# Softmax-gradient kernel on one core: a longer y buffer with the two groups of a pair shifted by 3840 columns, and ScalarE's row sum in one in-place instruction

## The chip, the cores and the metric

The kernel runs on one core of one Trainium2 chip. The metric is the device time of one execution in microseconds (us); smaller is better. Before the change the median was 1867.82 us in three runs (1866.99 to 1868.07).

Some words first. A *DMA* moves data between HBM (the main memory) and SBUF (on-chip memory); 16 DMA engines carry it in *packets* of 32 or 64 KB. A DMA *lands* when its completion reaches those who wait for it. VectorE and ScalarE do the arithmetic; SyncE only issues the DMAs. PSUM is a second on-chip memory, to which the old sum writes.

## The reference

```python
# y, dy: float32 [8, 1024, 8192]
softmax_x = np.exp(y)
sum_dy = np.sum(dy, axis=-1, keepdims=True)
return dy - softmax_x * sum_dy
```

There are 8192 rows of 8192 numbers. Each output element needs one exp, one multiply and one add; each row of dy must be summed first. y and dy are each read once (268.4 MB each), the output is written once (268.4 MB).

## The kernel before

A *group* is 128 partitions with two rows (R = 2) of 8192 columns each: 8 MB of dy in a tile `x`, 8 MB of y in `y_t`. The loop takes a *pair* of groups: two `x` tiles and a single `y_t`, which the first group fills with one load and the second with two loads, one a row, as the first group's arithmetic releases the columns. There are 16 pairs. Every DMA is issued by SyncE on one queue, in program order, and each waits on SyncE for what it depends on.

```python
    PIECES = [(0, 2048), (2048, 5120), (5120, D)]          # D = 8192
    x_ts = [pool.tile([P, W], fp32, name=f"x{j}") for j in range(2)]   # W = 2 * D
    y_t = pool.tile([P, W], fp32, name="y_t")
    copied = psum.tile([P, H], fp32, name="copied")         # H = D // 2, in PSUM

    def sums(x):                  # row 0 on VectorE, row 1 on ScalarE, in two halves
        ...
        nc.vector.tensor_reduce(out=s_t[:, 0:1], in_=x[:, :D], ..., negate=True)
        for h in range(2):
            nc.scalar.activation(
                copied[:], x[:, D + h * H : D + (h + 1) * H], COPY, accum_out=half_t[:, h : h + 1]
            )
        nc.vector.tensor_scalar(...)          # -(half 0 + half 1)
        return s_t

    def compute(x, s_t, r):       # one row, in three pieces
        for b, e in PIECES:
            cs = slice(r * D + b, r * D + e)
            nc.scalar.activation(y_t[:, cs], y_t[:, cs], EXP)
            nc.vector.scalar_tensor_tensor(out=x[:, cs], in0=y_t[:, cs],
                scalar=s_t[:, r : r + 1], in1=x[:, cs], op0=ALU.mult, op1=ALU.add)

    for g in range(0, G, 2):
        load_dy(g, x_ts[0])
        load_y(g, 0, W)
        s_t = sums(x_ts[0])
        for r in range(R):
            compute(x_ts[0], s_t, r)
        load_dy(g + 1, x_ts[1])
        s_t = sums(x_ts[1])
        for r in range(R):
            load_y(g + 1, r * D, (r + 1) * D)
            compute(x_ts[1], s_t, r)
        for j in range(2):
            nc.sync.dma_start(out=out_v[g + j], in_=x_ts[j][:])
```

Of the kernel before, what the change touches and what calls it, by code (L numbers as in the profile page):

```python
# [1 line left out]

# [5 lines left out]


EXP = mybir.ActivationFunctionType.Exp  # L10
COPY = mybir.ActivationFunctionType.Copy
ALU = mybir.AluOpType


@with_exitstack
def kernel(
    ctx: ExitStack,
    tc: tile.TileContext,
    y: bass.AP,
    dy: bass.AP,  # L20
    out: bass.AP,
):




    nc = tc.nc
    P = nc.NUM_PARTITIONS
    fp32 = mybir.dt.float32

    N, D = y.flatten_outer_dims().shape
    R = 2
    W = R * D
    G = N // (P * R)
    assert N == G * P * R and D == 8192 and G % 2 == 0
    H = D // 2

    PIECES = [(0, 2048), (2048, 5120), (5120, D)]

    y_v = y.flatten_outer_dims().rearrange("(g p r) d -> g p (r d)", p=P, r=R)  # L40
    dy_v = dy.flatten_outer_dims().rearrange("(g p r) d -> g p (r d)", p=P, r=R)
    out_v = out.flatten_outer_dims().rearrange("(g p r) d -> g p (r d)", p=P, r=R)

    pool = ctx.enter_context(tc.tile_pool(name="pool", bufs=1))
    stats = ctx.enter_context(tc.tile_pool(name="stats", bufs=3))
    psum = ctx.enter_context(tc.tile_pool(name="psum", bufs=1, space=bass.MemoryType.PSUM))
    x_ts = [pool.tile([P, W], fp32, name=f"x{j}") for j in range(2)]
    y_t = pool.tile([P, W], fp32, name="y_t")
    copied = psum.tile([P, H], fp32, name="copied")

    def load_dy(g, x):
        nc.sync.dma_start(out=x[:], in_=dy_v[g])  # L52

    def sums(x):
        s_t = stats.tile([P, R], fp32, name="s_t")
        half_t = stats.tile([P, 2], fp32, name="half_t")
        nc.vector.tensor_reduce(  # L57
            out=s_t[:, 0:1], in_=x[:, :D], axis=mybir.AxisListType.X, op=ALU.add, negate=True
        )
        for h in range(2):  # L60
            nc.scalar.activation(  # L61
                copied[:], x[:, D + h * H : D + (h + 1) * H], COPY, accum_out=half_t[:, h : h + 1]
            )
        nc.vector.tensor_scalar(  # L64
            out=s_t[:, 1:2],
            in0=half_t[:, 0:1],
            scalar1=half_t[:, 1:2],
            scalar2=-1.0,
            op0=ALU.add,
            op1=ALU.mult,  # L70
        )
        return s_t

    def load_y(g, lo, hi):
        nc.sync.dma_start(out=y_t[:, lo:hi], in_=y_v[g][:, lo:hi])  # L75

    def compute(x, s_t, r):
        for b, e in PIECES:
            cs = slice(r * D + b, r * D + e)
            nc.scalar.activation(y_t[:, cs], y_t[:, cs], EXP)  # L80
            nc.vector.scalar_tensor_tensor(  # L81
                out=x[:, cs],
                in0=y_t[:, cs],
                scalar=s_t[:, r : r + 1],
                in1=x[:, cs],
                op0=ALU.mult,
                op1=ALU.add,
            )

    for g in range(0, G, 2):  # L90
        load_dy(g, x_ts[0])
        load_y(g, 0, W)
        s_t = sums(x_ts[0])
        for r in range(R):
            compute(x_ts[0], s_t, r)
        load_dy(g + 1, x_ts[1])
        s_t = sums(x_ts[1])
        for r in range(R):
            load_y(g + 1, r * D, (r + 1) * D)
            compute(x_ts[1], s_t, r)  # L100
        for j in range(2):
            nc.sync.dma_start(out=out_v[g + j], in_=x_ts[j][:])


# [1 line left out]
_INS = ['y', 'dy']  # L106
_OUTS = [((8, 1024, 8192), 'float32')]


# [23 lines left out]
```

## Time and profile before

| what | before |
|---|---|
| median time | 1867.8 us |
| bytes moved | 805.37 MB, mean 432 GB/s |
| DMA queue busy, of 16 engines' span | 99.9% |
| VectorE (DVE), ScalarE (ACT) busy | 46%, 37% |
| period of one pair (from one load of the first x to the next) | 116.2 us |

These are lines of the page of the kernel before: the span, the busy engines, the rate in 40 equal slices of the span, the DMA queue with packets, MB and the share of 16 engines' time that its packets took, then the two lines of the chain that ended last (by engine, by tile), and last the DMA issues with their median us from issue to landing.

```profile
span 1865.9 us, 923 instructions
DVE 859.8 (46%) x256; ACT 698.7 (37%) x321; POOL 0.2 (0%) x4
...
GB/s 427 424 430 427 430 447 427 427 431 445 427 427 441 426 437 434 438 431 427 437 438 429 433 428 440 434 431 437 425 438 436 433 436 425 439 433 436 434 428 391
...
q1 hardware_dynamic: 16128, 805.31, 99.9%
...
DMA 64%; DVE 13%; ACT 10%; another core or an unknown queue 9%; issue 1%; SPq 0%; DVEq 0%; ACTq 0%
...
y_t<-in_y_dram SPq DMA_DIRECT2D x32, 4096.0 KB, 18.1
```

Two lines compete for the reader's belief. The queue line says that the DMA engines were busy for all but 0.1% of the span, at an even rate. The chain line gives 23% of the span to VectorE and ScalarE. A chain of waits follows one order of events back from the end; where several things go on at once it passes through one of them, and its share is not time that would be saved.

The next lines are SyncE's issues of one pair, in order of time: start in us, duration, engine and line, tile, and how many.

```profile
449.94 0.34 SPq L52 DMA_DIRECT2D x<-in_dy_dram  x1
450.38 0.75 SPq L75 DMA_DIRECT2D y_t<-in_y_dram  x1
469.39 0.33 SPq L52 DMA_DIRECT2D x<-in_dy_dram  x1
519.38 9.25 SPq L75 DMA_DIRECT2D y_t<-in_y_dram  x2
528.68 29.86 SPq L102 DMA_DIRECT2D out_dram<-x  x2
566.10 0.34 SPq L52 DMA_DIRECT2D x<-in_dy_dram  x1
```

The second x lands at 527.3 us. The first row load of y (519.38) is in the queue 8 us before that, so the engines go on to it without a pause. The same is true of each other issue in the pair (the shortest distance is that of the second store, 7.9 us). I call this distance, from an issue to the landing of the transfer ahead of it, the *lead*.

SyncE's own waits (who was waited for: us in total, times, longest) and the groups of ScalarE's sum (busy us, mean ns of one, idle before) are:

```profile
SPq L75 <- DVE x L81: 319.6, 32, 11.4
```

```profile
L61 ACT ACTIVATE copied<-x 128x4096 f32<-128x4096 f32 x64 | 229.6, 3587 | 864.9 <-DMA x<-in_dy_dram 863.9
L61 ACT ACTIVATION_READ_ACCUMULATOR copied<-x 128x1 f32 x64 | 11.9, 186 | 0.0
L64 DVE TENSOR_SCALAR s_t<-half_t 128x1 f32<-128x1 f32 x32 | 6.5, 204 | 0.0
```

SyncE waits for VectorE before the row loads of y, 10 us each on average. ScalarE's two half sums cost about 7.5 us a group, in a stretch where ScalarE otherwise waits for DMA.

### The profile page before, as it was taken

The numbers are of one execution on the slowest core, as the hardware profiler recorded it, in microseconds if no ns is written. First come the engines' busy times: TensorE is split into PE (matmuls) and PEld (weight loads), VectorE is DVE, ScalarE is ACT, GpSimd is POOL, SyncE is SP. The second block draws the span as 40 slices with busy tenths as digits, with TensorE's granted clock in tenths as the row PEclk, the third lists the DMA queues.
The fourth block names the chain that finished last, engine by engine and source line by source line (L and its number), as shares of the span: only waits on it lengthen the run. The fifth ranks groups of instructions, "written<-read, shape, count | busy, mean of one in ns | idle before, by whom it ended". The sixth has DMA issues, their size and how long they took to land.

```text
span 1865.9 us, 923 instructions
## 1 busy us (share of the span) xinstructions
DVE 859.8 (46%) x256; ACT 698.7 (37%) x321; POOL 0.2 (0%) x4
## 2 busy tenths in 40 slices
DVE  2907429074290732807328073280632806338063
ACT  2606326063260532605336052360523605236052
POOL 0000000000000000000000000000000000000000
DMA  9999999999999999999999999999999999999999
GB/s 427 424 430 427 430 447 427 427 431 445 427 427 441 426 437 434 438 431 427 437 438 429 433 428 440 434 431 437 425 438 436 433 436 425 439 433 436 434 428 391
DMA packets 16135, 805.37 MB, mean 432 GB/s; under 512 B 1792, under 2 KB 1792, under 8 KB 1792
## 3 DMA queue, kind: packets, MB, share of 16 engines
q1 hardware_dynamic: 16128, 805.31, 99.9%
q14 instruction: 7, 0.06, 0.0%
HBM read 536.87 MB, written 268.44 MB: 432 GB/s over the span
## 4 chain that ended last, share of the span: by engine, by line
DMA 64%; DVE 13%; ACT 10%; another core or an unknown queue 9%; issue 1%; SPq 0%; DVEq 0%; ACTq 0%
DMA x<-in_dy_dram 31%; DMA out_dram<-x 30%; DVE x L81 13%; ACT copied L61 6%; ACT y_t L80 4%; DMA y_t<-in_y_dram 3%; SPq L75 0%; DVEq L128 0%; ACTq L128 0%; SPq L52 0%; ACTq L80 0%; ACTq L61 0%
## 5 line engine op out<-in xcount | busy, mean ns | idle before, releaser
L81 DVE SCALAR_TENSOR_TENSOR x<-y_t,s_t,x 128x3072 f32<-128x3072 f32 (+1 forms) x192 | 579.4, 3059 | 255.7 <-ACT y_t L80 255.7
L57 DVE TENSOR_REDUCE s_t<-x 128x1 f32<-128x8192 f32 x32 | 277.8, 8682 | 722.3 <-DMA x<-in_dy_dram 722.3
L80 ACT ACTIVATE y_t<-y_t 128x3072 f32<-128x3072 f32 (+1 forms) x192 | 460.1, 2466 | 269.4 <-DMA y_t<-in_y_dram 253.2
L61 ACT ACTIVATE copied<-x 128x4096 f32<-128x4096 f32 x64 | 229.6, 3587 | 864.9 <-DMA x<-in_dy_dram 863.9
L61 ACT ACTIVATION_READ_ACCUMULATOR copied<-x 128x1 f32 x64 | 11.9, 186 | 0.0
L64 DVE TENSOR_SCALAR s_t<-half_t 128x1 f32<-128x1 f32 x32 | 6.5, 204 | 0.0
L61 ACT ACT_TABLE_LOAD x1 | 1.3, 1283 | 0.7 <-PEq L117 0.7
L117 POOL MEMSET const-bfloat16-1.0<- 128x1 bf16 x1 | 0.1, 101 | 0.0
L117 POOL MEMSET const-uint8-127<- 128x1 uint8 x1 | 0.1, 101 | 0.0
L117 POOL MEMSET const-float32-0.0<- 128x1 f32 x1 | 0.1, 98 | 0.2 <-issue 0.2
L117 POOL MEMSET const-float32-1.0<- 128x1 f32 x1 | 0.1, 98 | 0.0
## 6 DMA issues: line engine op xcount, KB each, us to landing
y_t<-in_y_dram SPq DMA_DIRECT2D x32, 4096.0 KB, 18.1
x<-in_dy_dram SPq DMA_DIRECT2D x32, 48.3
out_dram<-x SPq DMA_DIRECT2D x32, 32.5
y_t<-in_y_dram SPq DMA_DIRECT2D x16, 57.6
```

The lines of the kernel that those rows point to most:

```text
L57: nc.vector.tensor_reduce(out=s_t[:, 0:1], in_=x[:, :D], axis=mybir.AxisListType.X, op=ALU.add, negate=True)
L61: nc.scalar.activation(copied[:], x[:, D + h * H : D + (h + 1) * H], COPY, accum_out=half_t[:, h : h + 1])
L64: nc.vector.tensor_scalar(out=s_t[:, 1:2], in0=half_t[:, 0:1], scalar1=half_t[:, 1:2], scalar2=-1.0, op0=ALU.add, op1=ALU.mult,)
L80: nc.scalar.activation(y_t[:, cs], y_t[:, cs], EXP)
L81: nc.vector.scalar_tensor_tensor(out=x[:, cs], in0=y_t[:, cs], scalar=s_t[:, r : r + 1], in1=x[:, cs], op0=ALU.mult, op1=ALU.add,)
L117: nc = _bacc.Bacc("TRN2", target_bir_lowering=False, num_devices=1)
```

## The change

The intent: put y of the first group 3840 columns further into a longer buffer, so that the second group's y overlaps less of it and its row loads can be issued sooner; cut the first group's pieces at the new borders; and replace ScalarE's two half sums into PSUM by one instruction that copies the row onto itself.

```diff
-    PIECES = [(0, 2048), (2048, 5120), (5120, D)]
+    SHIFT = 3840
+    PIECES_A = [(0, 1024), (1024, D - SHIFT), (D - SHIFT, D)]
+    PIECES_B = [(0, 2048), (2048, 5120), (5120, D)]
...
-    y_t = pool.tile([P, W], fp32, name="y_t")
-    copied = psum.tile([P, H], fp32, name="copied")
+    y_t = pool.tile([P, SHIFT + W], fp32, name="y_t")
...
-        for h in range(2):
-            nc.scalar.activation(
-                copied[:], x[:, D + h * H : D + (h + 1) * H], COPY, accum_out=half_t[:, h : h + 1]
-            )
+        nc.scalar.activation(x[:, D:], x[:, D:], COPY, accum_out=second_t[:])
         nc.vector.tensor_scalar(
-            ... in0=half_t[:, 0:1], scalar1=half_t[:, 1:2], scalar2=-1.0, op0=ALU.add, op1=ALU.mult
+            out=s_t[:, 1:2], in0=second_t[:], scalar1=-1.0, scalar2=None, op0=ALU.mult
         )
...
-        load_y(g, 0, W)
+        load_y(g, SHIFT, 0, W)
...
-            compute(x_ts[0], s_t, r)
+            compute(x_ts[0], s_t, SHIFT, r, PIECES_A)
...
-            load_y(g + 1, r * D, (r + 1) * D)
-            compute(x_ts[1], s_t, r)
+            load_y(g + 1, 0, r * D, (r + 1) * D)
+            compute(x_ts[1], s_t, 0, r, PIECES_B)
```

`load_y` and `compute` take the extra offset, and the PSUM pool goes; nothing else changes.

More of the change, by code (lines that the diff above doesn't have):

```diff
@@ L35 @@
     assert N == G * P * R and D == 8192 and G % 2 == 0
-    H = D // 2
-    PIECES = [(0, 2048), (2048, 5120), (5120, D)]
+    SHIFT = 3840
+    PIECES_A = [(0, 1024), (1024, D - SHIFT), (D - SHIFT, D)]
+    PIECES_B = [(0, 2048), (2048, 5120), (5120, D)]
     y_v = y.flatten_outer_dims().rearrange("(g p r) d -> g p (r d)", p=P, r=R)
@@ L45 @@
     stats = ctx.enter_context(tc.tile_pool(name="stats", bufs=3))
-    psum = ctx.enter_context(tc.tile_pool(name="psum", bufs=1, space=bass.MemoryType.PSUM))
     x_ts = [pool.tile([P, W], fp32, name=f"x{j}") for j in range(2)]
-    y_t = pool.tile([P, W], fp32, name="y_t")
-    copied = psum.tile([P, H], fp32, name="copied")
+    y_t = pool.tile([P, SHIFT + W], fp32, name="y_t")
     def load_dy(g, x):
@@ L55, in sums @@
         s_t = stats.tile([P, R], fp32, name="s_t")
-        half_t = stats.tile([P, 2], fp32, name="half_t")
+        second_t = stats.tile([P, 1], fp32, name="second_t")
         nc.vector.tensor_reduce(
@@ L59, in sums, with load_y, compute @@
         )
-        for h in range(2):
-            nc.scalar.activation(
-                copied[:], x[:, D + h * H : D + (h + 1) * H], COPY, accum_out=half_t[:, h : h + 1]
-            )
+        nc.scalar.activation(x[:, D:], x[:, D:], COPY, accum_out=second_t[:])
         nc.vector.tensor_scalar(
-            out=s_t[:, 1:2],
-            in0=half_t[:, 0:1],
-            scalar1=half_t[:, 1:2],
-            scalar2=-1.0,
-            op0=ALU.add,
-            op1=ALU.mult,
-        )
-        return s_t
-    def load_y(g, lo, hi):
-        nc.sync.dma_start(out=y_t[:, lo:hi], in_=y_v[g][:, lo:hi])
-    def compute(x, s_t, r):
-        for b, e in PIECES:
-            cs = slice(r * D + b, r * D + e)
-            nc.scalar.activation(y_t[:, cs], y_t[:, cs], EXP)
+            out=s_t[:, 1:2], in0=second_t[:], scalar1=-1.0, scalar2=None, op0=ALU.mult
+        )
+        return s_t
+    def load_y(g, at, lo, hi):
+        nc.sync.dma_start(out=y_t[:, at + lo : at + hi], in_=y_v[g][:, lo:hi])
+    def compute(x, s_t, at, r, pieces):
+        for b, e in pieces:
+            xs = slice(r * D + b, r * D + e)
+            ys = slice(at + r * D + b, at + r * D + e)
+            nc.scalar.activation(y_t[:, ys], y_t[:, ys], EXP)
             nc.vector.scalar_tensor_tensor(
-                out=x[:, cs],
-                in0=y_t[:, cs],
+                out=x[:, xs],
+                in0=y_t[:, ys],
                 scalar=s_t[:, r : r + 1],
-                in1=x[:, cs],
+                in1=x[:, xs],
                 op0=ALU.mult,
```

## The prediction

> **What bounds the kernel now.** The DMA engines. The page shows queue 1 busy for 99.9% of 16 engines' span and 39 of 40 slices at 424 to 447 GB/s. 805.37 MB at the mean 432 GB/s is 1864 us of the 1865.9 us span. The Trainium skill ("DMA: Bandwidth & Descriptors", Specifications) gives a fabric ceiling of 435 GB/s and an HBM limit of about 358 GB/s per core; the trace sits at the first and exceeds the second. A 64 KB packet takes 2418 ns in the median: 434 GB/s for 16 engines. VectorE is busy 46%, ScalarE 37%.
>
> The chain of waits names VectorE (13%) and ScalarE (10%), but that is order, not time lost. In one pair (timeline, 450 to 566 us) the queue always holds the next transfer: x of the second group lands at 527.3, while the first y row was issued at 519.4; its second row at 528.3 (first row lands near 537); the first store at 528.7 (second row lands near 546.8); the second store at 558.5 (first store lands at 566.1). The smallest margin is about 7.5 us. A pair takes 116.2 us; 50.33 MB at 434 GB/s take 116.0.
>
> **What the change does.**
> - Shift and pieces. The second group's first y row overlaps only the first two pieces (4352 columns) of the first group's y instead of 8192. From VectorE's two sizes (2350 ns for 2048 columns, 3414 for 3072) I estimate 1.29, 3.68 and 4.21 us for 1024, 3328 and 3840: 9.2 us a row, as now. VectorE starts 0.85 us sooner (ScalarE's first piece is about 1.06 us, not 1.905), and its second piece ends 7.7 us after y lands instead of 11.5 for all three: both y row loads are issued 3 to 4 us sooner, and wait in the queue as much longer. Nothing lands sooner.
> - ScalarE's sum: one instruction of 8192 for two of 4096 (3587 ns) and two accumulator reads (186 ns). Estimate 7.1 instead of 7.55 us a group, 13 us in all, off the critical path. Writing into SBUF instead of PSUM should cost no more: copy and exp lie on one line of ns against columns. "SBUF — State Buffer" (SBUF: two separate sides) says engine ports and DMA ports cannot contend; exps in place during loads show no clear loss here.
> - The VectorE negation stays one instruction of about 204 ns.
> - No byte, packet size or issue count changes.
>
> On the critical path: nothing that matters. Packet time above the usual 2418 and 1213 ns is only about 4.6 us per engine in all, so no reordering wins more than about 0.3%. Start (first load lands at 22.7 us) and end keep their shape.
>
> **Predicted: 1867.2 us, 80% range 1864.5 to 1869.5.** Faster by over 2%: 1%; within 2%: 98%; slower by over 2%: 1%.
>
> **What would show it.** Queue 1 still at about 99.9%, 432 GB/s, period 116.1 to 116.3 us. SyncE's wait for VectorE before the y row loads shrinks by 3 to 4 us a pair or more (now 319.6 us over 32 waits); the row loads' median from issue to landing (18.1 us) rises by 3 to 4. ScalarE busy falls from 698.7 to about 686 us, VectorE stays near 860.
>
> **What would make it wrong.** SBUF placement or in-place ScalarE writes changing packet times (64 KB median over 2430 ns); the overlap being tracked more coarsely than by columns, so that a row load waits for the whole first group and the queue runs dry by up to 10 us a pair (slices under 420 GB/s); or the slow 32 KB packets (mean 1226 against 1213) vanishing, worth up to 3 us.

## The result, and the profile after

The changed kernel took 1868.09 us in the median of six runs (1866.49 to 1868.41), the kernel before 1867.53 us (1866.81 to 1868.07). The ratio is 1.0002 with a 95% interval of 0.9989 to 1.0015: the same time. Ratios here are the mean time of one kernel's fast runs over that of the other's fast runs of the same rounds, so they are not quite the ratio of the medians quoted.

The page of the changed kernel:

```profile
span 1866.1 us, 843 instructions
DVE 857.9 (46%) x256; ACT 689.3 (37%) x257; POOL 0.2 (0%) x4
...
GB/s 427 427 427 427 431 444 429 427 434 443 427 434 438 425 435 442 428 429 431 440 431 430 438 427 436 437 440 427 430 438 435 428 437 428 438 435 434 434 428 386
...
q1 hardware_dynamic: 16128, 805.31, 99.8%
...
DMA 65%; DVE 14%; another core or an unknown queue 10%; ACT 9%; issue 0%; DVEq 0%; ACTq 0%; SPq 0%
...
y_t<-in_y_dram SPq DMA_DIRECT2D x32, 4096.0 KB, 22.1
```

The queue is as full as before and moves the same bytes at the same rate. The last line says what the earlier issue bought: the row loads take 22.1 us from issue to landing instead of 18.1. They enter the queue 3 to 4 us sooner and stand in it as much longer.

SyncE's issues in the same pair of the changed kernel, its wait for VectorE, and the groups of the new sum:

```profile
450.09 0.34 SPq L52 DMA_DIRECT2D x<-in_dy_dram  x1
450.53 0.83 SPq L67 DMA_DIRECT2D y_t<-in_y_dram  x1
469.45 0.33 SPq L52 DMA_DIRECT2D x<-in_dy_dram  x1
516.17 9.25 SPq L67 DMA_DIRECT2D y_t<-in_y_dram  x2
529.22 29.78 SPq L95 DMA_DIRECT2D out_dram<-x  x2
566.55 0.34 SPq L52 DMA_DIRECT2D x<-in_dy_dram  x1
```

```profile
SPq L67 <- DVE x L74: 260.4, 32, 8.6
```

```profile
L60 ACT ACTIVATE x<-x 128x8192 f32<-128x8192 f32 x32 | 225.0, 7030 | 863.2 <-DMA x<-in_dy_dram 863.2
L60 ACT ACTIVATION_READ_ACCUMULATOR x<-x 128x1 f32 x32 | 6.0, 187 | 0.0
L61 DVE TENSOR_SCALAR s_t<-second_t 128x1 f32<-128x1 f32 x32 | 4.6, 143 | 0.0
```

The first row load goes out at 516.17 instead of 519.38, SyncE waits 59 us less for VectorE before the row loads (3.7 us a pair), and ScalarE's page total falls by 9 us. The wait has only moved: before the stores SyncE now waits 60 us longer for VectorE (466.3 us before, 526.6 after). Yet the next pair starts at the same time: 566.55 against 566.10, nearly in step with where each trace's pair began (450.09 and 449.94). Over the pairs after the first, the mean period is 116.3 us in both traces.

A table of the single packets in the trace makes the account exact. For each trace I summed the durations of the 32 KB and 64 KB packets and divided by 16 engines. "Slow" is the part of it above the usual 1213 ns (32 KB) and 2418 ns (64 KB); "idle" is the time from the first packet's start to the last one's end minus all packet time (a small negative value is overlap at the borders of packets). All in us per engine over the whole kernel:

```
kernel             packet time   slow   idle
before                  1862.7    4.6    0.2
after                   1862.3    4.2    0.9
```

Five microseconds of 1868 are neither bytes at the usual rate nor the kernel's start and end. A reordering that leaves the usual packet times, the start and the end as they are can't win more; what sets the usual packet time no run here tested.

### The profile page after: what moved, and what is told of

Read it like the earlier page. It is cut to its first block, busy times and chain, and to the rows that moved or that the text cites. A ratio compares the mean times of both kernels' runs of the same rounds, so it can differ in the third digit from the quotient of the medians.

```text
span 1866.1 us, 843 instructions
## 1 busy us (share of the span) xinstructions
DVE 857.9 (46%) x256; ACT 689.3 (37%) x257; POOL 0.2 (0%) x4
## 4 chain that ended last, share of the span: by engine, by line
DMA 65%; DVE 14%; another core or an unknown queue 10%; ACT 9%; issue 0%; DVEq 0%; ACTq 0%; SPq 0%
DMA x<-in_dy_dram 31%; DMA out_dram<-x 30%; DVE x L74 14%; ACT x L60 6%; ACT y_t L73 3%; DMA y_t<-in_y_dram 3%; DVEq L121 0%; ACTq L121 0%; SPq L52 0%; ACTq L73 0%; ACTq L60 0%
## 5 line engine op out<-in xcount | busy, mean ns | idle before, releaser
L74 DVE SCALAR_TENSOR_TENSOR x<-y_t,s_t,x 128x1024 f32<-128x1024 f32 (+2 forms) x192 | 579.4, 3059 | 257.5 <-ACT y_t L73 257.5
L73 ACT ACTIVATE y_t<-y_t 128x1024 f32<-128x1024 f32 (+2 forms) x192 | 460.1, 2466 | 280.0 <-DMA y_t<-in_y_dram 280.0
L60 ACT ACTIVATE x<-x 128x8192 f32<-128x8192 f32 x32 | 225.0, 7030 | 863.2 <-DMA x<-in_dy_dram 863.2
L60 ACT ACTIVATION_READ_ACCUMULATOR x<-x 128x1 f32 x32 | 6.0, 187 | 0.0
L61 DVE TENSOR_SCALAR s_t<-second_t 128x1 f32<-128x1 f32 x32 | 4.6, 143 | 0.0
## 6 DMA issues: line engine op xcount, KB each, us to landing
y_t<-in_y_dram SPq DMA_DIRECT2D x32, 4096.0 KB, 22.1
```

What stands on the lines that cost most here:

```text
L60: nc.scalar.activation(x[:, D:], x[:, D:], COPY, accum_out=second_t[:])
L61: nc.vector.tensor_scalar(out=s_t[:, 1:2], in0=second_t[:], scalar1=-1.0, scalar2=None, op0=ALU.mult)
L73: nc.scalar.activation(y_t[:, ys], y_t[:, ys], EXP)
L74: nc.vector.scalar_tensor_tensor(out=x[:, xs], in0=y_t[:, ys], scalar=s_t[:, r : r + 1], in1=x[:, xs], op0=ALU.mult, op1=ALU.add,)
```

## Experiments

The theory: the DMA engines always have a packet to move, so neither an earlier issue nor less ScalarE work shows. The rivals: (a) the shift gains and the in-place sum loses as much; (b) the arithmetic in the chain of waits is time of the kernel; (c) the issues have so much room that the shift could never matter.

### Each part alone

Run e1 is the changed kernel with the old sum put back:

```diff
...
-        nc.scalar.activation(x[:, D:], x[:, D:], COPY, accum_out=second_t[:])
+        for h in range(2):
+            nc.scalar.activation(
+                copied[:], x[:, D + h * H : D + (h + 1) * H], COPY, accum_out=half_t[:, h : h + 1]
+            )
...
```

> The longer y buffer and the new pieces, with ScalarE's two half sums into PSUM as before. Theory (the DMA engines are never without a packet, so nothing off them counts): 1866 to 1869 us, ratio 0.998 to 1.002; row loads issued 3 us earlier per pair as in the changed kernel, row-load time to landing about 22 us. Rival (a gain of the shift cancelled by a loss of the in-place sum): clearly faster than before, under 1862 us.

Measured: 1867.27 us, ratio 1.0002 (0.9985 to 1.0018). Row loads took 22.0 us to landing.

Run e2 is the kernel before with the new sum alone (the same edit the other way round, layout and pieces of before).

> The in-place sum alone, y layout and pieces as before. Theory: 1866 to 1869 us, 64 KB packets still at a median of 2418 ns, ScalarE busy near 689 us. Rival (cancellation): clearly slower than before, over 1873 us, with 64 KB packets slower.

Measured: 1866.99 us, ratio 1.0000 (0.9985 to 1.0015). The median 64 KB packet stayed at 2418 ns, ScalarE at 689.3 us. Neither part gains or loses; there is nothing to cancel, and rival (a) falls.

### No arithmetic at all

Run e3 keeps all loads and stores of the kernel before and drops the rest, so it stores dy.

```diff
         load_dy(g, x_ts[0])
         load_y(g, 0, W)
-        s_t = sums(x_ts[0])
-        for r in range(R):
-            compute(x_ts[0], s_t, r)
         load_dy(g + 1, x_ts[1])
-        s_t = sums(x_ts[1])
         for r in range(R):
             load_y(g + 1, r * D, (r + 1) * D)
-            compute(x_ts[1], s_t, r)
```

> All loads and stores of before in their order and sizes, no arithmetic at all; stores dy, a wrong result on purpose. Theory: 1862 to 1868 us, at most 0.3% under before. Rival (the 23% of the chain that VectorE and ScalarE hold are time that could be saved): well under 1800 us, down to about 1440.

Measured: 1866.06 us, ratio 0.9995 (0.998 to 1.001). Its page:

```profile
span 1864.3 us, 172 instructions
...
q1 hardware_dynamic: 16128, 805.31, 99.9%
...
y_t<-in_y_dram SPq DMA_DIRECT2D x32, 4096.0 KB, 33.7
```

All of VectorE's and ScalarE's work together costs about 1 us, which is within the noise. The 23% of the chain were order, not cost, and rival (b) falls. The last line adds the extreme case of an earlier issue: with no arithmetic to wait for, the row loads stand 33.7 us in the queue, and nothing is won. For these inputs the comparison doesn't notice that the subtracted product is missing, so a "correct" here says little about the arithmetic.

### The same work in an idle stretch

Run e7 adds one VectorE reduce of 6500 columns (6.91 us, result unused) to the kernel before, right after the first group's sums:

```diff
         s_t = sums(x_ts[0])
+        idle_t = stats.tile([P, 1], fp32, name="idle_t")
+        nc.vector.tensor_reduce(
+            out=idle_t[:], in_=x_ts[0][:, :6500], axis=mybir.AxisListType.X, op=ALU.add
+        )
```

> The kernel before with the same reduce, right after the sums of the first group, where VectorE waits 12.5 us for y. Theory: 1866 to 1869 us. Rival (VectorE's work in the chain is time of the kernel): 1867 + 16 x 6.9 = 1977 us.

Measured: 1867.22 us, ratio 1.0001 (0.9986 to 1.0016). Its page:

```profile
DVE 969.1 (52%) x272; ACT 698.7 (37%) x321; POOL 0.2 (0%) x4
```

VectorE is busy 109 us longer, and the time is the same.

### How much room there is, and what the shift adds to it

The next runs put extra VectorE work where it delays an issue. In e5 and e6 the reduce of 6500 columns stands after the first piece of the first group's first row, in the kernel before and in the changed one.

The edit of e5 (e6 has the same lines with the changed kernel's arguments):

```diff
-    def compute(x, s_t, r):
-        for b, e in PIECES:
+    def compute(x, s_t, r, extra=0):
+        for k, (b, e) in enumerate(PIECES):
...
+            for _ in range(extra if k == 0 else 0):
+                idle_t = stats.tile([P, 1], fp32, name="idle_t")
+                nc.vector.tensor_reduce(
+                    out=idle_t[:], in_=x[:, :6500], axis=mybir.AxisListType.X, op=ALU.add
+                )
...
-            compute(x_ts[0], s_t, r)
+            compute(x_ts[0], s_t, r, 1 if r == 0 else 0)
```

> The kernel before, with one more VectorE reduce of 6500 columns (about 6.9 us, result unused) after the first piece of each first group's first row. Theory: it moves the first y row load of the second group from 519.4 to about 526.3 us in the pair shown, 1.0 us ahead of the landing of x at 527.3[...]: about 1.7 us without packets a pair, some slow packets, 1867 + 27 = about 1895 us (1880 to 1930). Rival (y row loads are issued with slack to spare, the shift can't matter even for slower arithmetic): 1867 us.

> The same extra reduce at the same place in the changed kernel. Theory: the first y row load moves from 516.2 to about 523.1, still 4 us ahead; the second store is issued near 563.5, 3 us ahead: 1867 to 1875 us, at least 15 us under the run with the reduce in the kernel before. Rival (the shift buys no room): as slow as that run.

Measured: e5 1940.26 us, ratio 1.0391 (1.0375 to 1.0406), above the range expected. e6 1873.32 us, ratio 1.0029 (1.0004 to 1.0054), with runs from 1866.86 to 1876.81. Why e5 overshot is seen in the order in which the build put the instructions: the reduce reads columns that the second piece overwrites, and the build moved row 1's first piece ahead of row 0's second. The row load was late by the reduce and by that piece; its issue came 0.9 us after x had landed. The same happened in e6 with a smaller piece. The pair is not quite a fair one.

So e11 and e12 use six reduces of 1024 columns, 6.85 us together, which leave the order as it was (in both traces the reduces are followed by the second piece of the same row). The edit of e11:

```diff
...
+            for _ in range(extra if k == 0 else 0):
+                idle_t = stats.tile([P, 1], fp32, name="idle_t")
+                nc.vector.tensor_reduce(
+                    out=idle_t[:], in_=x[:, :1024], axis=mybir.AxisListType.X, op=ALU.add
+                )
...
-            compute(x_ts[0], s_t, r)
+            compute(x_ts[0], s_t, r, 6 if r == 0 else 0)
```

> The kernel before with six reduces of 1024 columns (about 6.9 us together) after the first piece of the first group's first row. They read only columns of that piece, so the build leaves the other pieces in their order, which it did not in e5. Theory: the first y row load is issued near 526.3 us instead of 519.4, 1.0 us ahead of x's landing: about 1 us a pair without packets and 1.5 us of slow packets, 1867 + 40 = about 1907 us (1885 to 1930). Rival (the 73 us of e5 came from the changed order alone): under 1875 us.

> The changed kernel with the same six reduces. Theory: first y row load near 521.5 to 523 us, 4 to 6 us ahead, second store about 3 us ahead: 1866 to 1880 us, with runs that differ as those of e6. Rival (the shift buys no room): as slow as the run with the six reduces in the kernel before.

Measured: e11 1912.86 us, ratio 1.0249 (1.0231 to 1.0266); e12 1867.91 us, ratio 1.0006 (0.9991 to 1.0021). The same extra work costs 46 us in the kernel before and nothing in the changed one; so of the 73 us of e5 the changed order explains only a part. Queue line and SyncE's issues of one pair in e11 (its trace lies later in time):

```profile
q1 hardware_dynamic: 16128, 805.31, 99.0%
```

```profile
535.78 9.25 SPq L75 DMA_DIRECT2D y_t<-in_y_dram  x2
545.08 26.59 SPq L107 DMA_DIRECT2D out_dram<-x  x2
578.42 0.34 SPq L52 DMA_DIRECT2D x<-in_dy_dram  x1
```

and in e12:

```profile
q1 hardware_dynamic: 16128, 805.31, 99.9%
```

```profile
520.72 9.25 SPq L67 DMA_DIRECT2D y_t<-in_y_dram  x2
533.77 26.96 SPq L100 DMA_DIRECT2D out_dram<-x  x2
566.04 0.34 SPq L52 DMA_DIRECT2D x<-in_dy_dram  x1
```

In e11 x lands at 537.3, so the lead of the row load has shrunk from 8 us to 1.5. The packets show the gap: 14 of the 16 engines end x's last packet between 535.4 and 535.9, the other two at 536.1 and 536.8, and the row load's first packets start between 536.7 and 537.7. In e12 the lead is still about 6 us.

Two more runs tell which part of the change gives the room: the reduce of e5 and e6 in the kernel with the shift alone (e9) and in that with the sum alone (e10).

> Shift and pieces without the new sum, with the extra reduce of the runs e5 and e6. Theory (the room for slower arithmetic comes from the shift and its pieces): 1867 to 1880 us, as e6. Rival (it comes from the in-place sum): near 1940 us, as e5.

> The in-place sum without shift and pieces, with the same extra reduce. Theory: 1930 to 1945 us, as e5. Rival: 1867 to 1880 us, as e6.

Measured: e9 1872.83 us (1866.86 to 1884.70), ratio 1.0039 (0.9997 to 1.0082); e10 1941.11 us, ratio 1.0395 (1.0378 to 1.0413). The room comes from the shift and its pieces, none of it from the sum. (The trace of e9 is of its fastest run, so no trace shows its slow ones.) Rival (c) falls too: the shift does matter once arithmetic is slower.

### Where the shift gives no room

Run e8 puts the reduce into the second group's first row of the changed kernel, where it delays the second store. `compute` is edited as in e6; the call differs:

```diff
...
-            compute(x_ts[1], s_t, 0, r, PIECES_B)
+            compute(x_ts[1], s_t, 0, r, PIECES_B, 1 if r == 0 else 0)
```

> The changed kernel with the same reduce in the second group's first row instead. Theory: the shift gives no room here; the second store is issued near 565.1 us, 1.4 us ahead of the first store's landing, so about 1.3 us a pair without packets and slow packets: 1867 + 20 = about 1890 us (1875 to 1930). Rival (the shift gives room at every point of the pair): 1867 us.

Measured: 1885.84 us, ratio 1.0098 (1.0081 to 1.0114).

```profile
q1 hardware_dynamic: 16128, 805.31, 99.9%
```

```profile
567.05 0.34 SPq L100 DMA_DIRECT2D out_dram<-x  x1
570.19 0.34 SPq L52 DMA_DIRECT2D x<-in_dy_dram  x1
```

The second store is issued at 567.05 in the pair shown, 3.1 us ahead of the first store's landing, on which the load of x at 570.19 waits (in the changed kernel without the reduce: 558.66, 7.9 us ahead). The time was as expected, the way was not: see the table below, where this run has no idle time at all. So the expectation's size was right by luck.

Run e4 asks the same from the other side: the changed kernel with one load for all of the second group's y, so that its arithmetic starts later.

```diff
+        load_y(g + 1, 0, 0, W)
         for r in range(R):
-            load_y(g + 1, 0, r * D, (r + 1) * D)
             compute(x_ts[1], s_t, 0, r, PIECES_B)
```

> The changed kernel, but y of the second group in one load of 64 KB rows instead of two of 32 KB rows. Theory: the arithmetic of the second group can start only when all of y is there, so the second store is issued about 9 us later than now, after the first store's packets have run out: 3 to 5 us without packets in each pair, 1867 + 16 x 4 = about 1930 us (1900 to 1955). Rival (only packet time counts): about 4 us faster than before, since the slow 32 KB packets go.

Measured: 1959.73 us, ratio 1.0496 (1.048 to 1.0512), in the direction of the theory, but 30 us above its figure and outside its range. The queue line and the end of one pair in SyncE's timeline: the second store (591.77) goes out only when the first has already landed, for the load of x that waited for that landing follows it directly.

```profile
q1 hardware_dynamic: 13824, 805.31, 97.0%
```

```profile
591.77 0.34 SPq L95 DMA_DIRECT2D out_dram<-x  x1
592.16 0.42 SPq L52 DMA_DIRECT2D x<-in_dy_dram  x1
```

### The account of the lost time

The same table as above, for the runs that matter:

```
kernel                   packet time   slow   idle   median us
before                        1862.7    4.6    0.2      1867.5
e3 no compute                 1861.6    3.5   -0.2      1866.1
e8 after, plus late           1880.2   22.2    0.0      1885.8
e11 before, six               1890.5   32.5   16.7      1912.9
e12 after, six                1862.7    4.7   -0.3      1867.9
e5 before, plus               1888.9   30.9   46.6      1940.3
e4 whole y                    1900.1   43.1   56.4      1959.7
```

For each run, slow plus idle, minus the 4.8 us of before, gives the time lost against before to within 2 us, except in e4, where the sum says 94.7 us and 92.2 were lost (its 64 KB rows save about a microsecond of the usual packet time). Idle engines are only one part of what a late issue costs here. The other is packets that take longer, and in e8 it is all of it. Where they lie, in the mean over pairs: in e8, 0.8 us in the last two packets of each engine before the turn from loads to stores and 0.4 us in the last packet of the second store; in e5, 0.5 us at the restart of the loads and 1.3 us before the turn to stores. My sizes for e4 and e5 left this part nearly out.

In e8 the slow packets are not at the late transfer itself. In the pair shown above, counting packets that are over 50 ns slow, those of the loads start at 545.7 to 549.0 us, 18 us or more before the late store is issued, while the first store has been in the queue since 531.71; the others start at 585.0 to 589.1. VectorE's extra reduce (544.3 to 551.2) can't be the whole cause: it is over long before 585, and in e7 and e12 such reduces run during loads with 4.0 and 4.7 us of slow time in all, no more than in before.

Pair by pair, the slow time per engine is:

```
pair                    1     2     3   ...   9    10    11    12    13    14    15    16
before               1.66  0.19  0.32  ...  0.25  0.19  0.14  0.26  0.08  0.19  0.06  0.31
e3 no compute        1.59  0.09  0.13  ...  0.13  0.16  0.15  0.09  0.09  0.10  0.11  0.11
e11 before, six      2.81  1.94  1.95  ...  1.97  1.88  2.01  1.97  1.97  1.89  2.07  1.90
e6 after, plus       1.92  0.08  0.28  ...  0.19  0.34  1.41  1.00  1.43  1.71  1.74  1.64
```

In every kernel here, even without arithmetic, the first pair has about 1.6 us or more of it, and in the undisturbed ones (before, after, e1, e2, e3, e7) each other pair has under 0.5. In e11, where the engines run dry in each pair, every pair has about 2 us. The run e6 changes over at its eleventh pair, which fits its runs that differ by 10 us. A second thing in the traces goes along with time: the 16 engines drift apart. In the kernel before they land one transfer within 0.7 us of each other in the first pair and within 3.9 us in the last, so that a lead that is enough for all engines early on may be too short for the fastest ones later. That would explain e6's change in mid-run (its spread has grown to 3.5 us by then), but no run changed the spread alone. It doesn't explain why turns are slow: the second pair of before has a spread of 0.7 us as the first, and a slow time of 0.19 us only, and e6's slow pairs have a wide spread. What makes a turn slow, and why a late issue elsewhere in the pair brings it on, stays open.

No experiment pointed to a kernel faster than both. The whole of the slow and idle time left is 5 us in 1868.

## Why the prediction was right

- *The DMA engines bound the kernel.* Shown in this sense: they always have a packet, without arithmetic the time is 1866.06 us, and with 109 us more VectorE work in an idle stretch it is 1867.22 us. What holds a 64 KB packet at 2418 ns (engine, path or memory) was not tested.
- *The chain's share of VectorE and ScalarE is order, not time.* Shown by the same two runs.
- *Row loads issued 3 to 4 us sooner, waiting as much longer.* Measured: 3.2 us sooner in the pair shown, 4.0 us longer to landing, the row load issued 7.67 us after ScalarE began on y (7.7 predicted for the end of VectorE's second piece), SyncE's wait before the row loads shorter by 3.7 us a pair.
- *Piece times.* Predicted 1.29, 3.68 and 4.21 us; measured 1.28, 3.68 and 4.21.
- *ScalarE's gain, 13 us, off the critical path.* The sign and the place were right; the size was 9.4 us, since the sum took 7.22 us a group (7.03 and 0.19 for its accumulator read) and not 7.1, and the page's busy time is not quite the sum of its groups (10.5 us less by groups). The negation took 143 ns instead of 204. Neither counts.
- *In-place writes do not disturb the DMA.* The Trainium skill says in "SBUF — State Buffer", section "SBUF: two separate sides", that engine ports and DMA ports cannot contend. The traces agree: the median 64 KB packet is 2418 ns in the kernels with the sum in PSUM, with the sum in place, and without arithmetic (means 2420.1, 2420.3 and 2420.1).
- *The total.* 1867.2 predicted (1864.5 to 1869.5), 1868.09 measured; the difference to before, 0.6 us, is within the runs' own spread.

One reading in the prediction was too easy: "the smallest margin is about 7.5 us" counts to the landing, as if an issue just before it were in time. Issue to first packet takes about 1.0 us in e11, the engines' last packets end up to 2 us before the landing is acted on, and a run whose shortest lead is 3 us (e8) has slow packets without any idle time. With about 6 us (e12, 5.7 for its second store) there was no loss, with about 5 (e6) some runs lost. It did not matter here, because both kernels keep about 8 us or more.

## What to carry to other kernels

When the DMA queue is busy for 99.9% of the span at an even rate, as here, earlier issues and cheaper arithmetic only lengthen the wait in the queue; before costing such a change, ask whether any engine-time without a packet is left to win. The room that an issue has is still worth knowing: it is what protects the kernel when arithmetic gets slower, and here a shift of 3840 columns made 6.9 us of extra work a pair free that cost the kernel before 46 us in all. Measure the room by adding work at the place in question, and check that the build keeps the order of the rest.

## What the Trainium skill lacked or had wrong

- "DMA: Bandwidth & Descriptors", section "Where 436 GB/s comes from": it says without a condition that for transfers between HBM and SBUF the HBM side, about 358 GB/s, binds, although the same paragraph calls its own measured 425 GB/s near the fabric rate. For this program, which runs on one core, the sentence does not hold: the core moved 432 GB/s over the span, reading 537 MB and writing 268 MB of HBM, close to the page's fabric ceiling of 435 GB/s.
- No page that I looked up says that packets can get slower in a pair with a late issue, most of all just before the queue turns from loads to stores: about 2 us an engine in each pair of e11 against under 0.5 in undisturbed pairs after the first; nor that the 16 engines drift apart, from 0.7 to 3.9 us between the landings of one transfer in the kernel before.
- "DMA: Bandwidth & Descriptors", section "Rules for kernel authors", advises to issue DMAs early, without a figure for how early is enough when the queue must not run dry. Here a shortest lead of 3 us went with a loss of about 18 us (e8), and in the four runs with about 6 us nothing was lost (e12).
